# Four instead of three of the eight quads of gate and up as seven block products, and the trunk's difference block written over the block it replaces

## The chip, the cores and the metric

The kernel runs as one program on one core of a Trainium2 chip. The metric is the device time of one launch in microseconds (us). The engines that matter here are TensorE (PE: matrix products, and PEld: its weight loads), VectorE (DVE: elementwise work on two operands), ScalarE (ACT: elementwise work on one operand) and the DMA queue of SyncE (SP), which brings the weights. Each engine works through its own list of instructions in order, and the lists meet in semaphores.

## The reference, cut to what matters

A trunk of two layers over 256 tokens of width 2048. Each layer has a mixer and then a SwiGLU, and it is the SwiGLU that the change touches:

```
x = x + swiglu(rmsnorm(x, g_ffn[layer]), w_gate[layer], w_up[layer], w_down[layer])
swiglu(h, w_gate, w_up, w_down) = (silu(h @ w_gate) * (h @ w_up)) @ w_down
# h: 256 x 2048;  w_gate, w_up: 2048 x 5632;  w_down: 5632 x 2048;  all float32
```

## The kernel before, in words

**Numbers.** Every float32 operand is split into a high part that TensorE takes exactly (`wh` for weights, written by ACT at L101) and the rest (`wl`, the raw weight minus `wh`, by DVE at L102). A product is three matmuls (L207 to L209): high by high, high by low, low by high. Six buffers of 128x1024 are there for `wh` and six for `wl`; a buffer comes free when the last matmul that reads it is done. Raw weights come in pieces of 1 MB into three `raw` buffers.

**Gate and up.** The 5632 hidden columns are taken in 11 blocks of 512 (index c), in parts of 4, 4 and 3 blocks (`PARTS`); behind each part comes the down projection of its hidden columns (`token_major`: four columns of 512, 24 matmuls for every 1 MB of weights). In a block, gate and up are computed together in eight *quads* (index j), one for every 256 rows of the weights. A quad is a 2 by 2 product of blocks: two token halves by two row groups, two row groups by gate and up. An *eight* (`quad_eight`) does it in 8 block products, 24 matmuls, from two pieces of weights of 128x1024. A *seven* (`quad_seven`) does it in 7 block products, 21 matmuls, after Winograd's form of Strassen's scheme. It needs sums of weight blocks first, by DVE: t1 and t3 in one subtraction of 128x1024 (L478), t2 (L480) and t4 (L481). Then it splits four pieces: P1 (b21 and b22, straight from `raw`), P2 (t2 and t4), P3 (b11, 128x512) and P4 (t1 and t3). It needs sums of trunk blocks as well (`forms`: s1 to s4), made once a layer in `put_pair`, where the normed trunk is turned and stored in `xs`.

Three of the sums of a seven go to PSUM tiles `c11`, `c12`, `c21` (pool `mm`, 4 buffers), four to `p1`, `p6`, `p5`, `p7` (pool `sm`, 4 buffers, which the transposes use too). At the end of a block comes its *epilogue*: five copies out of PSUM by ACT (L519), eight adds of 128x512 by DVE (L520), two SiLU by ACT (L573), two products by DVE (L575). The two halves of the hidden block are then turned by 8 transposes (L241) during the next block and split again, `hid` (L581 on ACT, L582 on DVE).

**Order.** `chunks_of` prepares the weights `AHEAD` = 2 quads ahead of the products. `next_pending` puts the transposes of the block before behind the products of quad 1. The final order on each engine is fixed when the program is built, by a scheduler that may move an instruction ahead of others; the engines then keep to it. In the profile a sum of weights at L478 and one at L481 both show as L475, the line of the helper `sub`.

Of the kernel before, what the change touches and what calls it, by code (L numbers as in the profile page):

```python
# [9 lines left out]
F32R = mybir.dt.float32r  # L10
AF = mybir.ActivationFunctionType
ALU = mybir.AluOpType
AX = mybir.AxisListType

P = 128
D = 2048
T = 256
KD = D // P
# [1 line left out]
NF = DFF // P  # L20
PARTS = (4, 4, 3)

SEVEN = (3, 5, 7)
AHEAD = 2
EPS = 1e-6
NH = 16
# [6 lines left out]
def trunk(ctx: ExitStack, tc: tile.TileContext, a: dict, out: bass.AP):  # L33
    nc = tc.nc
# [13 lines left out]
    def ev(shape, dtype=F32):  # L48

        return evs.tile([P, *shape], dtype, name="ev")  # L50
# [4 lines left out]
    pending = []  # L55
# [13 lines left out]
    def gain(name, i):  # L69
        return gains[:, g_at[name] + i:g_at[name] + i + 1]  # L70
# [173 lines left out]
    def into_trunk(w, k0, nk, moving, g, sums, chunks=None, scaled=None):  # L244


        def turn(m, src):

            def put(pt):
                for j in range(2):  # L250
                    split_into(xs[:, m + j, :], pt[:, j * T:(j + 1) * T], gain(g, m + j))

            def put_pair(pt):
                xg = ev([2, T])
                for j in range(2):
                    nc.scalar.activation(out=xg[:, j, :], in_=pt[:, j * T:(j + 1) * T], func=AF.Copy, scale=gain(g, m + j))
                nc.scalar.activation(out=xs[:, m:m + 2, :T], in_=xg, func=AF.Copy)
                nc.vector.tensor_tensor(out=xs[:, m:m + 2, T:], in0=xg, in1=xs[:, m:m + 2, :T].bitcast(F32), op=ALU.subtract)
                if m // 2 not in SEVEN:
                    return  # L260
                a11, a21, a12, a22 = xg[:, 0, :P], xg[:, 0, P:], xg[:, 1, :P], xg[:, 1, P:]
                f = ev([4, P])
                s1, s2, s3, s4 = (f[:, i, :] for i in range(4))
                nc.vector.tensor_tensor(out=s1, in0=a21, in1=a22, op=ALU.add)
                nc.vector.tensor_tensor(out=s2, in0=s1, in1=a11, op=ALU.subtract)
                nc.vector.tensor_tensor(out=s3, in0=a11, in1=a21, op=ALU.subtract)
                nc.vector.tensor_tensor(out=s4, in0=a12, in1=s2, op=ALU.subtract)
                q = scaled["forms"][:, SEVEN.index(m // 2), :, :, :]
                nc.scalar.activation(out=q[:, 0, :, :], in_=f, func=AF.Copy)
                nc.vector.tensor_tensor(out=q[:, 1, :, :], in0=f, in1=q[:, 0, :, :].bitcast(F32), op=ALU.subtract)  # L270

            turned(src, put_pair if scaled else put)

        def turn_scaled(c):
            xn = []

            def two(m):
                for t in range(2 if m == 0 else 0):
                    e = ev([512])
                    nc.scalar.activation(out=e, in_=x[:, t, c * 512:(c + 1) * 512], func=AF.Copy, scale=scaled["by"][:, t:t + 1])  # L280
                    xn.append(e)
                turn(4 * c + m, lambda t, j: xn[t][:, (m + j) * P:(m + j + 1) * P])

            pending.extend([lambda: two(0), lambda: two(2)])

        def evict(c, pss):
            s = slice(c * 512, (c + 1) * 512)
            for t in range(2):
                nc.vector.tensor_tensor(out=x[:, t, s], in0=pss[t], in1=x[:, t, s], op=ALU.add)
            if g is None:  # L290
                return
            for t in range(2):
                sq = ev([512])
                nc.scalar.activation(out=sq, in_=x[:, t, s], func=AF.Square, accum_out=sums[:, t, c:c + 1])
            if g == "final":
                for t in range(2):
                    nc.vector.tensor_tensor(out=x[:, t, s], in0=x[:, t, s], in1=gfin[:, s], op=ALU.mult)
            elif scaled is None:
                for m in (4 * c, 4 * c + 2):
                    pending.append(lambda m=m: turn(m, lambda t, j: x[:, t, (m + j) * P:(m + j + 1) * P]))  # L300
            elif c == 2:
                scaled["by"], scaled["back"] = trunk_rstd(sums[:, :, :3], 1536, back=True)
                for b in range(3):
                    turn_scaled(b)
            elif c == 3:
                turn_scaled(3)

        token_major(w, k0, nk, range(4), moving, evict, chunks)
# [15 lines left out]

    def forms():

        return big.tile([P, len(SEVEN), 2, 4, P], F32R, name="ckv")


    gfin = None  # L330
# [182 lines left out]
    def feed_forward(layer, sums, scaled, g_next):  # L513
# [7 lines left out]
        for part, n in enumerate(PARTS):  # L521
            hid = hidden()
            for c in range(n):

                c11, c12, c21, c22 = (ps_mm.tile([P, 512], F32, name="mm") for _ in range(4))
                open_ = set()

                def sum_into(ps, left, right, last):
                    token_product(ps, *left, *right, id(ps) not in open_, last)
                    open_.add(id(ps))  # L530

                for j in range(KD // 2):
                    w = next(chunks)
                    lasting = j == KD // 2 - 1
                    x11, x21, x12, x22 = ((xs[:, k, t * P:(t + 1) * P], xs[:, k, T + t * P:T + (t + 1) * P])
                                          for k in (2 * j, 2 * j + 1) for t in range(2))
                    if j not in SEVEN:
                        for xk, bg, bu in (((x11, x21), "b11", "b12"), ((x12, x22), "b21", "b22")):
                            for x_t, pg, pu in ((xk[0], c11, c12), (xk[1], c21, c22)):
                                sum_into(pg, x_t, w[bg], False)  # L540
                                sum_into(pu, x_t, w[bu], pu is c22 and xk[0] is x12 and j == max(set(range(KD // 2)) - set(SEVEN)))
                    else:
                        if j == SEVEN[0]:
                            p1, p6, p5, p7 = (ps_sm.tile([P, 512], F32, name="sm") for _ in range(4))
                        q = forms[:, SEVEN.index(j)]
                        s1, s2, s3, s4 = ((q[:, 0, i, :], q[:, 1, i, :]) for i in range(4))
                        sum_into(c11, x12, w["b21"], lasting)
                        sum_into(c12, s4, w["b22"], lasting)
                        sum_into(c21, x22, w["t4"], lasting)
                        sum_into(p1, x11, w["b11"], lasting)  # L550
                        sum_into(p6, s2, w["t2"], lasting)
                        sum_into(p5, s1, w["t1"], lasting)
                        sum_into(p7, s3, w["t3"], lasting)
                    if j in (1, 2):
                        next_pending(2)
                    if j == KD // 2 - 2:
                        e22 = copy(c22)
                if f is None:
                    f = stat.tile([P, 2], F32, name="factor")
                    nc.vector.tensor_tensor(out=f, in0=trunk_rstd(sums), in1=scaled["back"], op=ALU.mult)  # L560
                e11, e12, e21, u2 = copy(c11), copy(c12), copy(c21), copy(p6)
                u4 = ev([512])
                add(e11, p1, e11)
                add(u2, p1, u2)
                add(u4, p5, u2)
                add(u2, p7, u2)
                add(e21, u2, e21)
                add(u2, p5, u2)
                add(e12, u4, e12)
                add(e22, u2, e22)  # L570
                hd = []
                for t, (g, u) in enumerate(((e11, e12), (e21, e22))):
                    nc.scalar.activation(out=g, in_=g, func=AF.Silu, scale=f[:, t:t + 1])  # L573
                    h = qpool.tile([P, 512], F32, name="qn")
                    nc.vector.scalar_tensor_tensor(out=h, in0=u, scalar=f[:, t:t + 1], in1=g, op0=ALU.mult, op1=ALU.mult)  # L575
                    hd.append(h)
                for m in (0, 2):
                    def put(pt, hid=hid, m=4 * c + m):
                        pair = hid[:, m:m + 2, :]
                        src = pt.rearrange("p (j t) -> p j t", j=2)  # L580
                        nc.scalar.activation(out=pair[:, :, :T], in_=src, func=AF.Copy)  # L581
                        nc.vector.tensor_tensor(out=pair[:, :, T:], in0=src, in1=pair[:, :, :T].bitcast(F32), op=ALU.subtract)  # L582
                    pending.append(lambda m=m, hd=hd, put=put: turned(lambda t, j: hd[t][:, (m + j) * P:(m + j + 1) * P], put))
# [240 lines left out]
```

## Time and profile before

| | |
|---|---|
| median of 3 runs | 1942.32 us (1941.19 to 1942.67) |
| the profiled execution | 1942.75 us, of which the span from first to last instruction is 1940.9 us |
| TensorE | busy 99% of the span, weight loads 83%, granted clock 0.996 |
| VectorE, ScalarE | busy 75% and 55% |
| DMA | 371 MB, 191 GB/s |

A busy share is an average over stages. A "releaser" is what ended an engine's idle time before an instruction. Instructions overlap a little at their ends, so what one of them costs its engine is read from start to start, and that is called its pitch below. Consecutive equal instructions are merged in a timeline ("x2").

### The profile page before, as it was taken

What the parts mean: (1) busy time and instruction counts of PE and PEld (TensorE: products, weight loads), DVE (VectorE), ACT (ScalarE), POOL (GpSimd) and SP (SyncE); (2) the same over time, 40 slices, a digit from 0 to 9 for tenths busy, and PEclk for the clock granted to TensorE, in tenths of its full rate; (3) what the DMA queues carried; (4) which work ended last, traced back from release to release, by engine and by line L of the source; (5) the groups of instructions that cost most, each with busy time, mean ns of one, the idle gap of its engine ahead of it and who ended that gap; (6) DMA issues with size and microseconds to landing.
All of it is one profiled execution on the core that took longest, in us unless ns stands there. A gap on an engine that the chain in (4) does not pass through costs nothing.

```text
span 1940.9 us, 23494 instructions
## 1 busy us (share of the span) xinstructions
PE 1921.9 (99%) x9110; PEld 1610.7 (83%) x9110; DVE 1448.9 (75%) x1793; ACT 1066.0 (55%) x1424; POOL 10.1 (1%) x26
## 2 busy tenths in 40 slices
PE   9999999999999999999999999999999999999997
PEld 7888888888888888888889988888888888888886
DVE  6685589985688965887676755899856889658884
ACT  6554666563456643555554755665634566435562
POOL 0000000000000000000000000000000000000000
PEclk9999999999999999999999999999999999999998
DMA  8565545565555555456455235455655556655562
GB/s 310 174 215 197 195 160 209 195 213 194 179 195 195 210 201 190 179 195 217 175 194 175 96 135 184 171 208 188 214 194 183 187 199 211 210 181 177 208 242 87
DMA packets 54688, 370.94 MB, mean 191 GB/s; under 512 B 6320, under 2 KB 7856, under 8 KB 10544
## 3 DMA queue, kind: packets, MB, share of 16 engines
q1 hardware_dynamic: 52560, 364.93, 53.5%
q10 hardware_dynamic: 2016, 4.51, 0.6%
q8 instruction: 71, 1.16, 0.2%
q14 instruction: 41, 0.34, 0.0%
HBM read 367.32 MB, written 2.10 MB: 190 GB/s over the span
## 4 chain that ended last, share of the span: by engine, by line
PE 97%; DVE 1%; DMA 1%; ACT 1%; issue 0%; POOL 0%; ACTq 0%; SPq 0%; POOLq 0%
PE mm L207 24%; PE mm L209 24%; PE mm L208 24%; PE mm L131 5%; PE sm L209 3%; PE sm L208 3%; PE sm L207 3%; PE mm L132 2%; PE sm L241 2%; PE mm L363 1%; PE mm L364 1%; PE mm L137 1%; PE mm L362 1%; PE mm L136 1%; PE mm L138 1%; DMA raw<-in_w_v 1%
## 5 line engine op out<-in xcount | busy, mean ns | idle before, releaser
L102 DVE TENSOR_TENSOR wl<-raw,wh 128x1024 fp32r<-128x1024 f32 (+1 forms) x692 | 802.7, 1165 | 342.6 <-ACT wh L101 338.9
L101 ACT ACTIVATE wh<-raw 128x1024 fp32r<-128x1024 f32 (+1 forms) x692 | 695.1, 1013 | 538.4 <-PE mm L209 458.8
L207 PE MATMUL mm<-wh,xs 128*128 128x512 f32 x1012 | 395.2, 391 | 0.0
L209 PE MATMUL mm<-wh,xs 128*128 128x512 f32 x1012 | 393.9, 389 | 0.0
L208 PE MATMUL mm<-wl,xs 128*128 128x512 f32 x1012 | 393.8, 389 | 0.0
L207 PE MATMUL mm<-wh,hid 128*128 128x512 f32 x960 | 375.5, 391 | 0.0
L209 PE MATMUL mm<-wh,hid 128*128 128x512 f32 x960 | 373.6, 390 | 0.0
L208 PE MATMUL mm<-wl,hid 128*128 128x512 f32 x960 | 373.6, 389 | 0.0
L209 PEld LDWEIGHTS mm<-wh,xs 128*128 128x128 f32 x1012 | 189.9, 188 | 39.5
L207 PEld LDWEIGHTS mm<-wh,xs 128*128 128x128 f32 x1012 | 190.0, 188 | 39.0
L208 PEld LDWEIGHTS mm<-wl,xs 128*128 128x128 f32 x1012 | 190.0, 188 | 38.8
L209 PEld LDWEIGHTS mm<-wh,hid 128*128 128x128 f32 x960 | 180.2, 188 | 37.5
L207 PEld LDWEIGHTS mm<-wh,hid 128*128 128x128 f32 x960 | 180.2, 188 | 37.0 <-ACT hid L581 0.3
L208 PEld LDWEIGHTS mm<-wl,hid 128*128 128x128 f32 x960 | 180.3, 188 | 36.7
L102 DVE TENSOR_TENSOR wl<-sums,wh 128x1024 fp32r<-128x1024 f32 x132 | 161.3, 1222 | 63.6 <-ACT wh L101 63.6
L101 ACT ACTIVATE wh<-sums 128x1024 fp32r<-128x1024 f32 x132 | 139.4, 1056 | 126.1 <-DVE sums L475 96.6
L131 PE MATMUL mm<-xs,wh 128*128 128x512 f32 x375 | 133.8, 399 | 0.0
L132 PE MATMUL mm<-xs,wl 128*128 128x256 f32 x375 | 104.8, 280 | 0.0
L131 PEld LDWEIGHTS mm<-xs,wh 128*128 128x128 f32 x375 | 70.4, 188 | 15.9 <-DVE xs L170 0.3
L475 DVE TENSOR_TENSOR sums<-raw 128x1024 f32<-128x1024 f32 x66 | 80.5, 1220 | 1.0 <-DMA raw<-in_w_gu 0.5
L520 DVE TENSOR_TENSOR ev<-sm,ev 128x512 f32<-128x512 f32 x110 | 75.6, 688 | 2.6
L207 PE MATMUL sm<-wh,ckv 128*128 128x512 f32 x198 | 77.0, 389 | 0.0
(198 smaller groups left out, 1920.2 us busy)
## 6 DMA issues: line engine op xcount, KB each, us to landing
raw<-in_w_gu SPq DMA_DIRECT2D x176, 1024.0 KB, 4.8
raw<-in_w_d SPq DMA_DIRECT2D x88, 1024.0 KB, 4.8
raw<-in_w_o SPq DMA_DIRECT2D x32, 1024.0 KB, 4.8
raw<-in_w_v SPq DMA_DIRECT2D x11, 1024.0 KB, 6.6
raw<-in_w_z SPq DMA_DIRECT2D x8, 1024.0 KB, 5.0
raw<-in_w_u SPq DMA_DIRECT2D x8, 1024.0 KB, 4.8
raw<-in_w_q SPq DMA_DIRECT2D x6, 1024.0 KB, 4.9
raw<-in_w_ckv SPq DMA_DIRECT2D x4, 1024.0 KB, 4.8
```

The lines of the kernel that those rows point to most:

```text
L101: nc.scalar.activation(out=wh[:, :m], in_=raw[:, o:o + m], func=AF.Copy)
L102: nc.vector.tensor_tensor(out=wl[:, :m], in0=raw[:, o:o + m], in1=wh[:, :m].bitcast(F32), op=ALU.subtract)
L131: nc.tensor.matmul(ps, lhsT=wh, rhs=mv, start=first, stop=False)
L132: nc.tensor.matmul(ps[:, :T], lhsT=wl, rhs=mv[:, :T], start=False, stop=last)
L136: nc.tensor.matmul(ps[:, :T], lhsT=wh, rhs=mv[:, :T], start=first, stop=False)
L137: nc.tensor.matmul(ps[:, :T], lhsT=wh, rhs=mv[:, T:], start=False, stop=False)
L207: nc.tensor.matmul(ps, lhsT=hi, rhs=wh, start=first, stop=False)
L208: nc.tensor.matmul(ps, lhsT=hi, rhs=wl, start=False, stop=False)
L209: nc.tensor.matmul(ps, lhsT=lo, rhs=wh, start=False, stop=last)
L241: nc.tensor.transpose(pt[:, o:o + P], src(t, j), ident)
L475: sub = lambda out, p, q: nc.vector.tensor_tensor(out=out, in0=p, in1=q, op=ALU.subtract)
L520: add = lambda out, p, q: nc.vector.tensor_tensor(out=out, in0=p, in1=q, op=ALU.add)
```

## The change

`SEVEN` goes from quads 3, 5, 7 to quads 2, 4, 6, 7, so that a block has four sevens and four eights. In `put_pair`, the difference s3 = a11 - a21 is written over a21 before the trunk block is split, so that `xs` holds s3 where it held x21 (which a seven doesn't use) and `forms` holds three sums instead of four. The transposes of the block before are issued behind the quad ahead of the first seven (quad 1, as before), and `c22` is copied out behind quad 5 instead of 6.

```diff
-SEVEN = (3, 5, 7)
+SEVEN = (2, 4, 6, 7)
+EIGHT = tuple(j for j in range(KD // 2) if j not in SEVEN)
...
+                seven = m // 2 in SEVEN
+                if seven:
+                    a11, a21, a12, a22 = xg[:, 0, :P], xg[:, 0, P:], xg[:, 1, :P], xg[:, 1, P:]
+                    f = ev([3, P])
+                    s1, s2, s4 = (f[:, i, :] for i in range(3))
+                    nc.vector.tensor_tensor(out=s1, in0=a21, in1=a22, op=ALU.add)
+                    nc.vector.tensor_tensor(out=s2, in0=s1, in1=a11, op=ALU.subtract)
+
+                    nc.vector.tensor_tensor(out=a21, in0=a11, in1=a21, op=ALU.subtract)
+                    nc.vector.tensor_tensor(out=s4, in0=a12, in1=s2, op=ALU.subtract)
                 nc.scalar.activation(out=xs[:, m:m + 2, :T], in_=xg, func=AF.Copy)
                 nc.vector.tensor_tensor(out=xs[:, m:m + 2, T:], in0=xg, in1=xs[:, m:m + 2, :T].bitcast(F32), op=ALU.subtract)
-                if m // 2 not in SEVEN:
+                if not seven:
                     return
-                a11, a21, a12, a22 = xg[:, 0, :P], xg[:, 0, P:], xg[:, 1, :P], xg[:, 1, P:]
-                f = ev([4, P])
...
-        return big.tile([P, len(SEVEN), 2, 4, P], F32R, name="ckv")
+        return big.tile([P, len(SEVEN), 2, 3, P], F32R, name="ckv")
...
-                                sum_into(pu, x_t, w[bu], pu is c22 and xk[0] is x12 and j == max(set(range(KD // 2)) - set(SEVEN)))
+                                sum_into(pu, x_t, w[bu], pu is c22 and xk[0] is x12 and j == EIGHT[-1])
...
-                        sum_into(p7, s3, w["t3"], lasting)
-                    if j in (1, 2):
-                        next_pending(2)
-                    if j == KD // 2 - 2:
+                        sum_into(p7, x21, w["t3"], lasting)
+                    if j == SEVEN[0] - 1:
+                        next_pending(len(pending))
+                    if j == EIGHT[-1]:
                         e22 = copy(c22)
```

The order that the scheduler makes of it changes most around the end of a block. On DVE, before, at the end of layer 0's second block, the epilogue's adds (L520) stand among the splits of eights (`wl<-raw`), and the first seven's sums begin behind seven of the eight adds:

```order
L520 TENSOR_TENSOR ev<-sm,ev 128x512
L102 TENSOR_TENSOR wl<-raw,wh 128x1024
L520 TENSOR_TENSOR ev<-sm,ev 128x512 x2
L102 TENSOR_TENSOR wl<-raw,wh 128x1024
L520 TENSOR_TENSOR ev<-sm,ev 128x512
L520 TENSOR_TENSOR ev<-ev 128x512 x2
L575 SCALAR_TENSOR_TENSOR qn<-ev,factor 128x512
L520 TENSOR_TENSOR ev<-sm,ev 128x512
L102 TENSOR_TENSOR wl<-raw,wh 128x1024
L520 TENSOR_TENSOR ev<-ev 128x512
L475 TENSOR_TENSOR sums<-raw 128x1024
L575 SCALAR_TENSOR_TENSOR qn<-ev,factor 128x512
```

And now, at the same place (the lines have moved by one to four: L524 was L520, L103 was L102, L479 and L484 were L475 and L480, L579 was L575):

```order
L103 TENSOR_TENSOR wl<-raw,wh 128x1024 x4
L524 TENSOR_TENSOR ev<-sm,ev 128x512 x2
L479 TENSOR_TENSOR sums<-raw 128x1024
L524 TENSOR_TENSOR ev<-sm,ev 128x512
L103 TENSOR_TENSOR wl<-raw,wh 128x1024
L524 TENSOR_TENSOR ev<-sm,ev 128x512
L524 TENSOR_TENSOR ev<-ev 128x512 x2
L579 SCALAR_TENSOR_TENSOR qn<-ev,factor 128x512
L524 TENSOR_TENSOR ev<-sm,ev 128x512
L484 TENSOR_TENSOR sums<-sums,raw 128x512
L524 TENSOR_TENSOR ev<-ev 128x512
L479 TENSOR_TENSOR sums<-raw,sums 128x512
```

All four split pieces of the next block's quads 0 and 1 (x4) now stand ahead of the first add, and the epilogue is interleaved with the sums and the first split of quad 2, a seven.

On ACT, at the last quad of layer 0's second block, before: the four pieces of quad 7 (`raw_2812`, `sums_2814`), then the splits for the next block, and only then, among those, the copies of `c22`, `c11` and `c12` (`mm_2602`, `mm_2599`, `mm_2600`):

```order
L101 ACTIVATE wh_2816<-raw_2812 128x1024
L101 ACTIVATE wh_2822<-sums_2814 128x1024
L101 ACTIVATE wh_2826<-raw_2812 128x512
L101 ACTIVATE wh_2830<-sums_2814 128x1024
L101 ACTIVATE wh_2857<-raw_2855 128x1024
L101 ACTIVATE wh_2861<-raw_2855 128x1024
L519 ACTIVATE ev_2889<-mm_2602 128x512
L101 ACTIVATE wh_2893<-raw_2891 128x1024
L519 ACTIVATE ev_2922<-mm_2599 128x512
L101 ACTIVATE wh_2897<-raw_2891 128x1024
L519 ACTIVATE ev_2924<-mm_2600 128x512
```

And now (quad 7 is `raw_2837` and `sums_2839`; `mm_2618`, `mm_2615`, `mm_2616` are `c22`, `c11`, `c12`):

```order
L102 ACTIVATE wh_2841<-raw_2837 128x1024
L523 ACTIVATE ev_2883<-mm_2618 128x512
L523 ACTIVATE ev_2947<-mm_2615 128x512
L523 ACTIVATE ev_2949<-mm_2616 128x512
L102 ACTIVATE wh_2847<-sums_2839 128x1024
L102 ACTIVATE wh_2851<-raw_2837 128x512
L102 ACTIVATE wh_2855<-sums_2839 128x1024
L102 ACTIVATE wh_2887<-raw_2885 128x1024
L102 ACTIVATE wh_2891<-raw_2885 128x1024
```

The copies of the finished sums now stand between the first and the second piece of quad 7. On PE two products of quad 2 (into `p5` and `p7`) are moved behind the first half of quad 3.

## Rows read from the trace of the kernel before

**Rows 1.** The page: busy time, share of the span and instructions of each engine
```profile
PE 1921.9 (99%) x9110; PEld 1610.7 (83%) x9110; DVE 1448.9 (75%) x1793; ACT 1066.0 (55%) x1424; POOL 10.1 (1%) x26
```
**Rows 2.** Busy time in stretches: block four of layer 0, then one down column
```profile
core 0: us, PE busy (x) PEld busy (x) DVE busy (x) ACT busy (x) POOL busy (x), PEclk, DMA share, GB/s
374.88:417.26 42.38, 42.38 (x193) 35.18 (x192) 38.64 (x45) 25.35 (x32) 0.00 (x0) 1.00 0.56 199
440.75:462.51 21.76, 21.76 (x97) 18.02 (x97) 11.01 (x11) 8.49 (x8) 0.00 (x0) 1.00 0.58 195
```
**Rows 3.** Timeline of PE: block two, its transposes, block four (start, us, engine, line, op)
```profile
290.97 0.39 PE L207 MATMUL mm<-wh,xs 128*128 128x512 f32 x1
...
301.85 1.03 PE L241 MATMUL sm<-ident,qn 128*128 128x128 f32 x8
...
375.71 0.39 PE L207 MATMUL mm<-wh,xs 128*128 128x512 f32 x1
```
**Rows 4.** Groups by line: the first sums of all sevens
```profile
L475 DVE TENSOR_TENSOR sums<-raw 128x1024 f32<-128x1024 f32 x66 | 80.5, 1220 | 1.0 <-DMA raw<-in_w_gu 0.5
```
**Rows 5.** Timeline of DVE: an eight's and a seven's splits, second block of layer 0
```profile
307.77 1.22 DVE L102 TENSOR_TENSOR wl<-raw,wh 128x1024 fp32r<-128x1024 f32 x1
308.91 1.22 DVE L475 TENSOR_TENSOR sums<-raw 128x1024 f32<-128x1024 f32 x1
310.05 2.35 DVE L102 TENSOR_TENSOR wl<-raw,wh 128x1024 fp32r<-128x1024 f32 x2
312.32 0.68 DVE L480 TENSOR_TENSOR sums<-sums,raw 128x512 f32<-128x512 f32 x1
313.03 0.69 DVE L475 TENSOR_TENSOR sums<-raw,sums 128x512 f32<-128x512 f32 x1
314.94 1.22 DVE L102 TENSOR_TENSOR wl<-sums,wh 128x1024 fp32r<-128x1024 f32 x1 [1.21 <-ACT wh L101]
316.08 0.68 DVE L102 TENSOR_TENSOR wl<-raw,wh 128x512 fp32r<-128x512 f32 x1
316.68 1.22 DVE L102 TENSOR_TENSOR wl<-sums,wh 128x1024 fp32r<-128x1024 f32 x1
317.81 1.22 DVE L102 TENSOR_TENSOR wl<-raw,wh 128x1024 fp32r<-128x1024 f32 x1
```
**Rows 6.** Timeline of ACT: the high part of that seven's second piece, then a copy
```profile
313.84 1.06 ACT L101 ACTIVATE wh<-sums 128x1024 fp32r<-128x1024 f32 x1 [2.99 <-DVE sums L475]
...
331.23 0.58 ACT L519 ACTIVATE ev<-mm 128x512 f32<-128x512 f32 x1
331.70 1.06 ACT L101 ACTIVATE wh<-raw 128x1024 fp32r<-128x1024 f32 x1
```
**Rows 7.** Timeline of DVE: from an epilogue's first add to the split of hid
```profile
332.51 0.68 DVE L520 TENSOR_TENSOR ev<-sm,ev 128x512 f32<-128x512 f32 x1
333.11 1.22 DVE L102 TENSOR_TENSOR wl<-raw,wh 128x1024 fp32r<-128x1024 f32 x1
...
338.76 0.75 DVE L575 SCALAR_TENSOR_TENSOR qn<-ev,factor 128x512 f32<-128x512 f32 x1
339.42 0.68 DVE L520 TENSOR_TENSOR ev<-sm,ev 128x512 f32<-128x512 f32 x1
...
346.02 1.28 DVE L582 TENSOR_TENSOR hid<-sm,hid 128x512 fp32r<-128x512 f32 x2
347.29 1.23 DVE L102 TENSOR_TENSOR wl<-sums,wh 128x1024 fp32r<-128x1024 f32 x1
```
**Rows 8.** Timeline of DVE in the first block: trunk sums and an idle time
```profile
260.77 1.23 DVE L102 TENSOR_TENSOR wl<-sums,wh 128x1024 fp32r<-128x1024 f32 x1 [2.46 <-ACT wh L101]
...
264.45 0.28 DVE L264 TENSOR_TENSOR ev<-ev 128x128 f32<-128x128 f32 x1
264.65 1.22 DVE L102 TENSOR_TENSOR wl<-raw,wh 128x1024 fp32r<-128x1024 f32 x1
```
**Rows 9.** DMA issues: the weights of gate and up, median us to landing
```profile
raw<-in_w_gu SPq DMA_DIRECT2D x176, 1024.0 KB, 4.8
```

More of the change, by code (lines that the diff above doesn't have):

```diff
@@ L256, in put_pair @@
                     nc.scalar.activation(out=xg[:, j, :], in_=pt[:, j * T:(j + 1) * T], func=AF.Copy, scale=gain(g, m + j))
+                seven = m // 2 in SEVEN
[7 more added lines that the diff above has]
+                    nc.vector.tensor_tensor(out=s4, in0=a12, in1=s2, op=ALU.subtract)
                 nc.scalar.activation(out=xs[:, m:m + 2, :T], in_=xg, func=AF.Copy)
                 nc.vector.tensor_tensor(out=xs[:, m:m + 2, T:], in0=xg, in1=xs[:, m:m + 2, :T].bitcast(F32), op=ALU.subtract)
-                if m // 2 not in SEVEN:
+                if not seven:
                     return
-                a11, a21, a12, a22 = xg[:, 0, :P], xg[:, 0, P:], xg[:, 1, :P], xg[:, 1, P:]
-                f = ev([4, P])
[L263 to L267, printed above, removed]
                 q = scaled["forms"][:, SEVEN.index(m // 2), :, :, :]
@@ L545, in feed_forward @@
                         q = forms[:, SEVEN.index(j)]
-                        s1, s2, s3, s4 = ((q[:, 0, i, :], q[:, 1, i, :]) for i in range(4))
+                        s1, s2, s4 = ((q[:, 0, i, :], q[:, 1, i, :]) for i in range(3))
                         sum_into(c11, x12, w["b21"], lasting)
```

## The prediction

> **What bounds the kernel now.** I read the page's busy times first, then the same by stages, then the timelines of the engines that look full there. Over the whole span TensorE is the full engine: 99% busy, against 75% for DVE [rows 1]. By stages it looks different. In a block of gate and up DVE is busy 38.64 us of 42.38, in a down column 11.01 of 21.76 [rows 2]: the 75% is a mean over 91% and 51%, and the change works only where DVE is at 91%.
>
> TensorE's side of a block: from the start of block two to its transposes PE runs two eights, 48 matmuls, in 301.85 - 290.97 = 10.88 us, 0.2267 us each. Two blocks take 375.71 - 290.97 = 84.74, 42.37 each [rows 3]. The 183 matmuls of a block (5 x 24 + 3 x 21) make 41.49, which leaves 0.88 for the 8 transposes. So PE never waits there, and sets the pace.
>
> DVE's side. From the last split of one eight (307.77) to that of the next (317.81) lies one seven and one eight, 10.04 us, of which 1.21 is idle [rows 5]. The idle time is a relay: DVE makes t4 (313.03), ACT makes its high part (313.84, after it had waited 2.99 us for that sum) [rows 6], and DVE takes the low part at 314.94, 1.91 us after it began t4. Nothing else of DVE's list may pass. The parts by pitch: 1.14 us for 128x1024 (307.77 to 308.91), 0.60 for 128x512 (316.08 to 316.68) [rows 5]. So an eight costs DVE 2 x 1.14 = 2.28 and a seven 10.04 - 2.28 = 7.76, the relay included. On PE they cost 24 x 0.2267 = 5.44 and 4.76. A seven saves PE 0.68 us and costs DVE 5.48 more than the eight that it replaces; the question is only whether DVE has that to spare.
>
> **The change part by part.** *The products.* 66 sevens in 22 blocks [rows 4] become 88: PE loses 22 x 3 matmuls, 22 x 0.68 = 15.0 us. A block's PE work is then 41.69 us.
>
> *DVE's list of a block*, from the first add of an epilogue to the next one, in the new order. Quad 2, a seven, is now woven into the epilogue: 8 adds at 0.60 (332.51 to 333.11) and one product at 0.66 (338.76 to 339.42) [rows 7], the sum of 1024 and the split of P1 at 1.14, t2 at 0.60: 4.80 + 0.66 + 2.28 + 0.60 = 8.34 to the start of t4. Then the relay of 1.91, in which the second product fits. Then P2, P3, P4 at 1.14, 0.60, 1.14: 13.13. Quad 3, an eight: 15.41. The two splits of hid, 347.29 - 346.02 = 1.27 [rows 7]: 16.68. Quads 4 and 5: 10.04. Quads 6 and 7, two sevens running: 2 x 7.76 = 15.52. Quads 0 and 1 of the next block: 4.56. Sum 46.80 us, against 41.69 of PE. So where the list runs without a lead it is DVE that sets a block, and the block is 46.80 - 42.37 = 4.43 longer than now.
>
> The idle part of this is three relays of 1.21 and 0.64 in the epilogue: 4.27. It is the term not seen under this load; its ends are nothing (other work fills every wait; 42.53 for a block) and the full 4.27. I take the full value, because in the new order too the split of P2 stands right behind t4 in quads 4, 6 and 7, and in the row the engine idled just so.
>
> *The lead.* In a down column DVE has half its time free [rows 2], so each part begins with all six buffers full. First blocks (one in each of the three parts of each layer, six in all) have no epilogue in their list: 46.8 - 8 x 0.60 - 2 x 0.66 - 1.27 = 39.4 us, under PE's. They win 0.68 each. At the end of one, the last split for the next block's quad 1 needs the buffer of quad 7's P2, whose last reader is the fifth of seven products, 1.36 us before the block's end. ACT and DVE take about 1.0 and 1.14 for the split, with 0.2 to 0.3 for signals and then the last copies: the first adds go 1.3 us after the block's end. Before the change they went 0.8 before it (332.51, against 290.97 + 42.37 = 333.34) [rows 3, 7].
>
> In the steady state the adds come later. PE's last wait in a block is for the low part of quad 7's P2; 12 matmuls are left then, 2.72 us. DVE has P3, P4 and two eights left, 0.60 + 1.14 + 4.56 = 6.30. So the next epilogue starts 3.58 us after the block's end. Second blocks (six) begin with 1.3 in the place of 3.58 and so take 46.80 - 2.28 = 44.52, +2.15 each. Later blocks (2 + 2 + 1 in a layer, ten in all) take +4.43.
>
> *ACT's new order.* In quad 7 the copies of c11 and c12 stand ahead of the second piece. ACT can then split P2 only after PE has finished c12: 1.36 us into quad 7, about 0.35 for the result to land, 0.47 for the copy (331.23 to 331.70) [rows 6]. DVE's own t4 comes at about that time in the steady state, so I add nothing; alone it would hold PE about 2.7 us in a block, which is the stall that the list above already gives to quad 7.
>
> *Trunk sums.* A fourth pair per layer takes three or four DVE instructions of 0.20 (264.45 to 264.65) more and a split. The idle 2.46 us there hides it [rows 8]; without that cover it would cost some 1.4 us a layer. *Down projection.* An epilogue of 10.5 us behind a lag of 3.6 ends 14 us into a down column of 21.8, and the transposes stand later on PE by then. I take nothing; up to 1 us for each of six parts is in the range.
>
> **Sum.** 6 x (-0.68) + 6 x 2.15 + 10 x 4.43 = -4.1 + 12.9 + 44.3 = +53.1. The profiled execution's own time is 1942.75 us, 0.43 over the median: 1942.32 + 53.1 = 1995.4, I say **1996 us**. Its own range: the lag after a first block between 0.3 and 3.6 (six times) and half a microsecond on the list (sixteen times), 1982 to 2010.
>
> **The rivals.** *TensorE stays the bound.* Then the 15.0 us come off: 1927.3. For it speaks the page [rows 1]. The Trainium skill (Perfetto Trace Analysis, "Identifying the Most-Contended Engine") says to improve the engine with the highest occupancy, judging TensorE by its weight loads: 83% here against DVE's 75%, and by that rule the time would be this 1927.3. The stage disagrees: 35.18 us of weight loads against 38.64 of DVE in a block [rows 2]. It holds only if DVE finds 5.1 us in a block. Chance 0.05.
>
> *The waits are filled.* If ACT works so far ahead that no relay shows, DVE's list is 42.53, 0.84 over PE's 41.69. The lead of 3.58 - 1.3 = 2.28 us covers that for two blocks behind a first one. Time: 22 x (-0.68) and a few tenths in the last blocks, about 1929; with half the relays filled (44.7 a block, +2.3 in later blocks, nothing in second ones) 1942.3 - 4.1 + 23 = 1961. Against it: the sum t4 comes out of DVE itself right before. Chance 0.05 for the first, 0.06 for the second.
>
> *A ring of buffers is longer than DVE's list.* The transposes of hid hold two of four PSUM tiles until DVE has split them, 16.7 us into its list; now quad 2 needs those tiles, and its last two products wait. From there PE has 6 matmuls, half of quad 3 (2.72), quads 4, 5, 6 (14.96) and two products; then come a copy, a split on ACT and the remaining 7.4 of DVE: 16.7 + 1.4 + 2.7 + 15.0 + 1.4 + 1.9 + 7.4 = 46.5. That is only 0.3 under the list. A raw buffer is freed about 7 us before it is wanted, and a piece lands in 4.8 [rows 9]. If one of the two is 1.5 us longer than I count, sixteen blocks carry it: 2020. Chance 0.09.
>
> *The change doesn't do what it says*: no; the order shows 22 sevens more.
>
> **How the numbers follow.** The forecast has 0.75. The range 1958 to 2020 leaves out the two gains (0.10) and the far ends. "Same" (within 0.2%, 3.9 us, which is what a measurement of this kernel can tell from no change) lies between cases and gets 0.03; faster 0.10; slower 0.87.
>
> **What would show it right or wrong.** In the profile after: blocks of about 41.7, 44.5, 46.8, 46.8 us in a part of four, read from the transposes or the SiLUs; PE idle in front of quad 7's second piece, waiting for DVE's low part or ACT's high part; DVE over 90% busy in second to fourth blocks with idle times of 1.2 only behind t4; down columns unchanged at 21.8. It is wrong if second and later blocks take 42 us, if DVE's idle time behind t4 is gone, or if PE's wait is mostly for PSUM tiles or for `raw`.

## The result and the profile after

The changed kernel takes 2001.28 us in the median of four runs (2001.0 to 2004.2), the kernel before 1942.49 in the same comparison: a ratio of 1.0307, with a 95% interval of 1.0291 to 1.0322. 1996 had been forecast: slower, as forecast, and 5 us more than forecast. The profiled spans are 1999.4 and 1940.9 us, 58.5 apart.

Lines of the file moved by a few: what was L102 (low part), L475 (first sum), L480 (t4), L520 (epilogue's adds), L207 to L209 (three matmuls of a product) before is L103, L479, L484, L524, L208 to L210 now. First the page: the busy times, then the chain of work that ended last, by engine.

```profile
PE 1941.5 (97%) x9044; PEld 1601.0 (80%) x9044; DVE 1535.2 (77%) x1913; ACT 1094.0 (55%) x1470; POOL 10.1 (1%) x26
...
PE 62%; DVE 26%; issue 5%; ACT 4%; DMA 2%; ACTq 0%; SPq 0%; POOL 0%; POOLq 0%; DVEq 0%
```

PE has 66 matmuls less (9110 - 9044) and is busy 19.6 us longer than before [rows 1]; part of that is the granted clock, below. Over the whole span it still looks like the full engine, as DVE's 77% looks like room to spare. On the page only the chain tells that DVE carries a quarter of the time.

The same by stages: the gate and up blocks of the three parts of layer 0, with the columns as in [rows 2].

```profile
249.45:431.93 182.48, 174.97 (x754) 139.31 (x753) 163.76 (x194) 109.96 (x142) 0.69 (x1) 0.98 0.49 174
519.71:698.16 178.45, 171.86 (x747) 137.83 (x745) 158.19 (x177) 102.08 (x124) 0.00 (x0) 0.99 0.50 177
785.92:919.15 133.23, 128.85 (x559) 103.62 (x557) 117.25 (x130) 77.06 (x94) 0.00 (x0) 0.99 0.50 178
```

In the kernel before the same three stretches, cut at the same matmuls, are these, PE busy to the last hundredth:

```profile
248.37:418.09 169.72, 169.72 (x767) 140.88 (x765) 150.26 (x175) 105.29 (x133) 0.69 (x1) 1.00 0.53 189
506.09:674.95 168.86, 168.86 (x759) 140.06 (x757) 146.26 (x161) 98.09 (x118) 0.00 (x0) 1.00 0.54 192
762.94:889.43 126.49, 126.49 (x568) 104.88 (x566) 107.63 (x118) 72.78 (x87) 0.00 (x0) 1.00 0.54 190
```

The stretches became 12.8, 9.6 and 6.7 us longer; with layer 1 (11.8, 9.6, 6.7) that is 57.2 of the 58.5. A down stretch between them takes 87.8 us where it took 88.0. So the time is lost where the change is, and but for 1.3 us there alone.

The pace is DVE's. The first add of each epilogue of layer 0's first part, in DVE's timeline (start, length, line; what follows in brackets is the idle time before):

```profile
293.77 0.68 DVE L524 TENSOR_TENSOR ev<-sm,ev 128x512 f32<-128x512 f32 x1
...
340.56 0.68 DVE L524 TENSOR_TENSOR ev<-sm,ev 128x512 f32<-128x512 f32 x1
...
387.34 0.69 DVE L524 TENSOR_TENSOR ev<-sm,ev 128x512 f32<-128x512 f32 x1
...
434.13 0.68 DVE L524 TENSOR_TENSOR ev<-sm,ev 128x512 f32<-128x512 f32 x1
```

They are 46.79, 46.78 and 46.79 us apart; 42.37 before. The only idle times in the middle one of these cycles stand behind t4, in the epilogue 0.55, in quads 4, 6 and 7 1.20, 1.21 and 1.18; 4.14 together. The one of quad 7, and what DVE does behind it until the next epilogue:

```profile
376.06 1.22 DVE L479 TENSOR_TENSOR sums<-raw 128x1024 f32<-128x1024 f32 x1
377.32 0.69 DVE L484 TENSOR_TENSOR sums<-sums,raw 128x512 f32<-128x512 f32 x1
378.05 0.69 DVE L479 TENSOR_TENSOR sums<-raw,sums 128x512 f32<-128x512 f32 x1
379.92 1.23 DVE L103 TENSOR_TENSOR wl<-sums,wh 128x1024 fp32r<-128x1024 f32 x1 [1.18 <-ACT wh L102]
381.06 0.69 DVE L103 TENSOR_TENSOR wl<-raw,wh 128x512 fp32r<-128x512 f32 x1
381.66 1.22 DVE L103 TENSOR_TENSOR wl<-sums,wh 128x1024 fp32r<-128x1024 f32 x1
382.80 4.63 DVE L103 TENSOR_TENSOR wl<-raw,wh 128x1024 fp32r<-128x1024 f32 x4
```

ACT meanwhile: the copies of c11 and c12, then the high part of the sums, held up by t4 and not by the copies (0.24 us, releaser DVE). PE waits for that high part once in each of sixteen blocks, all but the first of a part. Below stand two rows of ACT, then two of PE, then the group of all such waits in the page.

```profile
377.31 1.28 ACT L523 ACTIVATE ev<-mm 128x512 f32<-128x512 f32 x2 [2.39 <-PE mm L210]
378.83 1.06 ACT L102 ACTIVATE wh<-sums 128x1024 fp32r<-128x1024 f32 x1 [0.24 <-DVE sums L479]
```
```profile
379.94 0.50 PE L208 MATMUL mm<-wh,xs 128*128 128x512 f32 x1 [1.98 <-ACT wh L102]
380.28 0.39 PE L208 MATMUL sm<-wh,ckv 128*128 128x512 f32 x1
```
```profile
L208 PE MATMUL mm<-wh,xs 128*128 128x512 f32 x880 | 342.1, 395 | 28.7 <-ACT wh L102 28.3
```

That is a chain of DVE (t4), ACT (high part), PE, with DVE idle for 1.2 us of it. The 28.3 us are not the loss: PE waits there because DVE's list is behind, and what PE waits in one place it does not wait in another.

### The profile page after: what moved, and what is told of

The parts are those of the page before. It is cut to its first block, busy times and chain, and to the rows that moved or that the text cites. A ratio compares the mean times of both kernels' runs of the same rounds, so it can differ in the third digit from the quotient of the medians.

```text
span 1999.4 us, 23599 instructions
## 1 busy us (share of the span) xinstructions
PE 1941.5 (97%) x9044; PEld 1601.0 (80%) x9044; DVE 1535.2 (77%) x1913; ACT 1094.0 (55%) x1470; POOL 10.1 (1%) x26
## 4 chain that ended last, share of the span: by engine, by line
PE 62%; DVE 26%; issue 5%; ACT 4%; DMA 2%; ACTq 0%; SPq 0%; POOL 0%; POOLq 0%; DVEq 0%
PE mm L209 15%; PE mm L210 15%; PE mm L208 15%; DVE wl L103 14%; DVE sums L479 4%; PE mm L132 4%; ACT wh L102 4%; DVE ev L524 3%; PE mm L133 2%; DVE sums L484 2%; PE sm L209 2%; PE sm L210 2%; PE sm L208 1%; DMA raw<-in_w_v 1%; DVE hid L586 1%
## 5 line engine op out<-in xcount | busy, mean ns | idle before, releaser
L103 DVE TENSOR_TENSOR wl<-raw,wh 128x1024 fp32r<-128x1024 f32 (+1 forms) x692 | 785.1, 1147 | 283.7 <-ACT wh L102 282.0
L102 ACT ACTIVATE wh<-raw 128x1024 fp32r<-128x1024 f32 (+1 forms) x692 | 676.7, 994 | 447.0 <-PE mm L210 360.8
L208 PE MATMUL mm<-wh,hid 128*128 128x512 f32 x960 | 375.1, 391 | 0.9 <-ACT hid L585 0.9
L209 PE MATMUL mm<-wl,hid 128*128 128x512 f32 x960 | 374.9, 391 | 0.0
L210 PE MATMUL mm<-wh,hid 128*128 128x512 f32 x960 | 374.2, 390 | 0.0
L208 PE MATMUL mm<-wh,xs 128*128 128x512 f32 x880 | 342.1, 395 | 28.7 <-ACT wh L102 28.3
L209 PE MATMUL mm<-wl,xs 128*128 128x512 f32 x880 | 349.7, 397 | 6.1 <-DVE wl L103 5.1
L210 PE MATMUL mm<-wh,xs 128*128 128x512 f32 x880 | 345.3, 392 | 0.0
L102 ACT ACTIVATE wh<-sums 128x1024 fp32r<-128x1024 f32 x176 | 185.5, 1054 | 231.7 <-DVE sums L479 200.1
L103 DVE TENSOR_TENSOR wl<-sums,wh 128x1024 fp32r<-128x1024 f32 x176 | 215.2, 1223 | 94.9 <-ACT wh L102 94.9
L208 PEld LDWEIGHTS mm<-wh,xs 128*128 128x128 f32 x880 | 165.3, 188 | 68.9 <-ACT wh L102 35.1
L208 PEld LDWEIGHTS mm<-wh,hid 128*128 128x128 f32 x960 | 180.3, 188 | 38.1 <-ACT hid L585 1.4
L209 PEld LDWEIGHTS mm<-wl,xs 128*128 128x128 f32 x880 | 165.8, 188 | 56.2 <-DVE wl L103 23.9
L210 PEld LDWEIGHTS mm<-wh,hid 128*128 128x128 f32 x960 | 180.3, 188 | 37.3
L209 PEld LDWEIGHTS mm<-wl,hid 128*128 128x128 f32 x960 | 180.4, 188 | 36.7
L210 PEld LDWEIGHTS mm<-wh,xs 128*128 128x128 f32 x880 | 166.1, 189 | 32.3
L479 DVE TENSOR_TENSOR sums<-raw 128x1024 f32<-128x1024 f32 x88 | 107.2, 1218 | 0.9 <-DMA raw<-in_w_gu 0.4
L523 ACT ACTIVATE ev<-mm 128x512 f32<-128x512 f32 x88 | 50.8, 586 | 52.4 <-PE mm L210 51.4
L524 DVE TENSOR_TENSOR ev<-sm,ev 128x512 f32<-128x512 f32 x110 | 73.6, 683 | 0.2
```

The lines of the kernel that those rows point to most:

```text
L102: nc.scalar.activation(out=wh[:, :m], in_=raw[:, o:o + m], func=AF.Copy)
L103: nc.vector.tensor_tensor(out=wl[:, :m], in0=raw[:, o:o + m], in1=wh[:, :m].bitcast(F32), op=ALU.subtract)
L208: nc.tensor.matmul(ps, lhsT=hi, rhs=wh, start=first, stop=False)
L209: nc.tensor.matmul(ps, lhsT=hi, rhs=wl, start=False, stop=False)
L210: nc.tensor.matmul(ps, lhsT=lo, rhs=wh, start=False, stop=last)
L479: sub = lambda out, p, q: nc.vector.tensor_tensor(out=out, in0=p, in1=q, op=ALU.subtract)
```

## The experiments

All but one are edits of the changed kernel; times beside them are of the same comparisons, where the kernel before ran at 1942.5 to 1942.8 us.

**Is it the fourth seven, or the rest of the edit?** The rest is the trunk's differences stored in place and the order that comes with it. (With three sevens the same code puts the transposes behind quad 2 and copies `c22` behind quad 6.)

```
-SEVEN = (2, 4, 6, 7)
+SEVEN = (3, 5, 7)
```

> The changed kernel with SEVEN = (3, 5, 7) again: only the difference stored in xs, the earlier sums in put_pair and the order around them stay. If DVE's list of a block is the cause, three sevens bring it back to about 41.4 us, under TensorE's 42.4: 1942 us, within 4. If the trunk's sums (made ahead of the split of xs, written in place) or the place of the transposes cost the time, a good part of the 59 us stays: 1960 us or more.

Measured: 1943.05, ratio 1.0002 [0.9992, 1.0011]. The stretches are those of before (168.86 and 126.49). The storing in place costs nothing; all is in the fourth seven and the places of the sevens, which this run does not separate.

**TensorE's buffers and products, or the sums on VectorE?** The matmuls of the changed kernel stay, the sums of weight blocks go; t1 to t4 are then split from raw weights in their place, so a part of the computation is left out.

```
-        sub(sums[:, :1024], raw[:, 512:1536], raw[:, :1024])
...
-        sub(t4, b[3], t2)
-        parts += split_raw(sums[:, 1024:], 1024)
+        parts += split_raw(raw[:, 1024:], 1024)
...
-        parts += split_raw(sums[:, :1024], 1024)
+        parts += split_raw(raw[:, :1024], 1024)
```

> The changed kernel without the sums of weight blocks: P2 and P4 are split from raw weights instead of t2, t4, t1, t3 (that part of the computation is left out); matmuls, splits and the epilogue stay. DVE's list falls by 3 x 3.74 + 2.99 = 14.2 us to about 32.6 a block, TensorE's 41.7 rule: the 15 us come off, 1927 to 1931 us. If TensorE waits for PSUM tiles held by the transposes, or for ACT's copies ahead of quad 7's second piece, the blocks stay near 46: 1985 us or more.

Measured: 1927.24, ratio 0.9924 [0.9909, 0.9938]. This is the gain of the products alone, and it came to 15.5 us (15.0 had been worked out from three matmuls in 22 blocks). PSUM tiles, raw buffers and ACT's copies are as in the changed kernel and hold up nothing here. By itself that does not exclude the ring of buffers, because DVE's work is a part of that ring and is shorter in this run too. But in the changed kernel PE's waits in these blocks are for weights (28.3 us for ACT's high parts, 5.1 for DVE's low parts) and, 2.0 us of them, of transposes for DVE's products; the profile puts none down to a PSUM tile or to `raw`. The next run leaves tiles and buffers as they are.

**How much of the loss is the relay?** In each seven the two sums that t4 needs go first, and the split of the raw half is issued behind t4. While ACT makes t4's high part, DVE then has that split to do. (The split is tied to t4, because the scheduler may move an instruction ahead of others.)

```
-        parts = split_raw(raw[:, 1024:], 1024)
         nc.vector.tensor_tensor(out=t2, in0=t3, in1=b[0], op=ALU.add)
-        sub(t4, b[3], t2)
+        last = sub(t4, b[3], t2)
+        with tc.issue_after(last.ins):
+            parts = split_raw(raw[:, 1024:], 1024)
```

> The changed kernel with the split of P1's low part queued on DVE behind the sum t4, so that it runs while ACT makes P2's high part. The same instructions, no work less. If DVE's list with its relays sets the block: the list falls by 3 x 1.14 + 0.65 = 4.1 us to 42.7, lag over TensorE's 41.7 grows by 1 us a block and the lead of 2.3 covers most of it: 1928 to 1938 us. If only DVE's work counted and the relays were filled already: no change, 2001 us. If PSUM tiles or ACT's copies set the block: within 10 us of 2001.

Measured: 1936.92, ratio 0.9971 [0.996, 0.9982]. Not an instruction fewer (DVE executes 1913, as in the changed kernel) and 64 us faster. DVE's timeline in quad 7 now (t2 is L483 here, and the epilogue's adds are L525):

```profile
365.76 1.22 DVE L479 TENSOR_TENSOR sums<-raw 128x1024 f32<-128x1024 f32 x1
367.02 0.69 DVE L483 TENSOR_TENSOR sums<-sums,raw 128x512 f32<-128x512 f32 x1
367.75 0.69 DVE L479 TENSOR_TENSOR sums<-raw,sums 128x512 f32<-128x512 f32 x1
368.36 1.22 DVE L103 TENSOR_TENSOR wl<-raw,wh 128x1024 fp32r<-128x1024 f32 x1
369.63 1.23 DVE L103 TENSOR_TENSOR wl<-sums,wh 128x1024 fp32r<-128x1024 f32 x1
370.78 0.68 DVE L103 TENSOR_TENSOR wl<-raw,wh 128x512 fp32r<-128x512 f32 x1
```

The bracket with the 1.2 us is gone. The adds of the epilogues are 43.13 us apart, from the second block of a part on:

```profile
333.91 0.69 DVE L525 TENSOR_TENSOR ev<-sm,ev 128x512 f32<-128x512 f32 x1
...
377.06 1.28 DVE L525 TENSOR_TENSOR ev<-sm,ev 128x512 f32<-128x512 f32 x2
```

A stretch of four blocks takes 167.79 us where it took 178.45 (before: 168.86). 46.78 - 43.13 = 3.65 of the 4.14 idle us of a cycle were won. Most of the rest is in these rows too: the sums' split starts 1.27 us after the raw one (368.36, 369.63), where 1.14 is the pitch, so 0.13 is left of the relay in each of three sevens; in the fourth a product of the epilogue stands between.

**The dose, from the other side.** In the kernel before, each seven's first sum is made twice.

```
         sub(sums[:, :1024], raw[:, 512:1536], raw[:, :1024])
+        sub(sums[:, :1024], raw[:, 512:1536], raw[:, :1024])
```

> The kernel before with one more VectorE instruction per seven (the subtraction of 1024 of L478, 1.14 us, issued twice with the same result), so 3.42 us more per block and not a matmul more. Theory (VectorE's in-order list bounds a block as soon as it is longer than TensorE's 42.37): the list of before is 41.4, it becomes 44.8, the steady cycle from block to block 44.8, ten later blocks of 2.4 and six second blocks of 0 to 2: 1962 to 1980. Rival (TensorE, 99% busy, is the bound and VectorE at 74% has room): 1942, no change.

Measured: 1971.21, ratio 1.0147 [1.0132, 1.0162]. Its later epilogues stand 44.99 and 45.15 apart, against 44.8 from the list. The kernel before had been less than 1 us per block from the point at which DVE takes over (1.0 by the list's 41.4 of 42.37, 0.6 to 0.8 by the measured cycles less 3.42); a stretch went from 168.86 to 174.27, with TensorE's work untouched.

**Another placement: three sevens at the end of a block.**

```
-SEVEN = (2, 4, 6, 7)
+SEVEN = (3, 5, 6, 7)
```

> The changed kernel with the four sevens at quads 3, 5, 6, 7. DVE's list has the same instructions and the same relays but one may be covered by the splits of hid: 45.5 to 46.8 a block, 1980 to 2003 us. If the PSUM tiles are the cause (the first seven stands right behind the transposes), it has an eight in between now, 5.4 us: then TensorE would wait less and the time would be under 1960 us.

Measured: 2040.35, ratio 1.05 [1.0484, 1.0516]. Both theories missed, the one that the other runs bear out by 37 us. The sums are the same and the matmuls are the same. A stretch of four took 187.01 us (178.45 in the changed kernel), 8.56 more. The rows of the first block of layer 0's second part, DVE's first add and PE's first matmul of the next block, tell a good part of it:

```profile
568.05 0.68 DVE L524 TENSOR_TENSOR ev<-sm,ev 128x512 f32<-128x512 f32 x1
```
```profile
565.22 0.39 PE L208 MATMUL mm<-wh,xs 128*128 128x512 f32 x1
```

and the same two in the changed kernel:

```profile
559.91 0.68 DVE L524 TENSOR_TENSOR ev<-sm,ev 128x512 f32<-128x512 f32 x1
```
```profile
560.74 0.39 PE L208 MATMUL mm<-wh,xs 128*128 128x512 f32 x1
```

With three sevens in a row, DVE ends even a first block 2.83 us behind PE, where it had been 0.83 ahead. The 8.56 us are: 0.54 in the first block itself, 3.66 of lead lost (2.83 + 0.83), 2.81 in the three cycles (47.68, 48.45 and 48.17 against 47.93, 46.78 and 46.78) and 1.55 at the end, where the last epilogue began 1.69 us behind the block instead of 3.24. Of the cycles' part, 0.65 in a cycle is the fourth relay, which stood in the epilogue in the changed kernel and cost 0.55 there; now all four cost 1.2 (4.79 idle, against 4.14). Two of the three cycles hold something more, the granted clock. PE waits in quad 6 already, the clock falls behind that wait, and PE is late with c12; ACT's copies of c11 and c12, which stand ahead of the high part of the sums, then hold that high part up, and DVE idles for 1.97 us instead of 1.18. The granted clock is 0.50 from 649.0 to 652.4. A row of ACT behind it and one of DVE:

```profile
654.51 1.28 ACT L523 ACTIVATE ev<-mm 128x512 f32<-128x512 f32 x2 [4.01 <-PE mm L210]
```
```profile
656.76 1.23 DVE L103 TENSOR_TENSOR wl<-sums,wh 128x1024 fp32r<-128x1024 f32 x1 [1.97 <-ACT wh L102]
```

So the new order on ACT, which costs nothing in the changed kernel (0.24 us to spare), costs 0.5 to 0.8 us in such a cycle.

**Relays or the run of sevens?** The same placement in the kernel with the filled relay.

```
-SEVEN = (2, 4, 6, 7)
+SEVEN = (3, 5, 6, 7)
```

> The sevens at 3, 5, 6, 7 (as in e5, 2040) with the relay filled (as in e3, 1937). Theory A (both the relay and the run of three sevens at a block's end count: in e5 the first block of a part already leaves VectorE 2.8 us late, where the changed kernel leaves it 0.8 us early): the cycle falls from 47.7 to 43.2, three later blocks of a part at 43.3 behind a first of 42.3, 172 per stretch of four against 167.8 in e3: 1950 to 1970. Theory B (e5 lost by the relays alone, none of its four standing in a block's end): 1935 to 1942.

Measured: 1954.64, ratio 1.0062 [1.0047, 1.0077], inside theory A and outside B. The relays were 86 of the 98 us by which e5 was above the kernel before; but with the relay gone the run of sevens still costs 18 us against e3 (1936.92): its stretch of four is 170.68 against 167.79. DVE ends a first block 2.36 us behind PE (551.51, 549.15), where in e3 it is 0.83 ahead. The reading is that three sevens in a row take 3 x (7.76 - 1.21) = 19.7 us on DVE's list and 14.3 on PE, and that the lead of two or three weight chunks does not cover the difference. The first seven has moved from quad 2 to quad 3 as well, with the transposes one quad later; no run tests that by itself.

**Taking more off VectorE: GpSimd.** In e3, the three adds of an epilogue that read no PSUM go to GpSimd.

```
+        held = lambda out, p, q: nc.gpsimd.tensor_tensor(out=out, in0=p, in1=q, op=ALU.add)
...
-                add(e21, u2, e21)
+                held(e21, u2, e21)
...
-                add(e12, u4, e12)
-                add(e22, u2, e22)
+                held(e12, u4, e12)
+                held(e22, u2, e22)
```

> The changed kernel with the relay filled (as in e3) and the three adds of a block's end that touch no PSUM on GpSimd instead of VectorE. Theory: VectorE's cycle of 43.13 loses 3 x 0.60 = 1.8 and falls to 41.3, under TensorE's 41.7; TensorE bounds every block and the time is 1928 to 1933. Rivals: GpSimd's add is slow or holds VectorE up (its only adds seen are 128x2 at 0.69 us), then the multiplications behind it (L579) wait on VectorE's queue and the time is 1937 to 1960, as e3 or worse; or TensorE's idle of e3 is not VectorE's, then 1937.

Measured: 1983.59, ratio 1.0213 [1.0196, 1.023]; the second of the outcomes, and beyond its end. The rows of GpSimd and of DVE in one epilogue (L526 is the add that GpSimd makes, L581 DVE's product):

```profile
337.95 2.85 POOL L526 TENSOR_TENSOR ev<-ev 128x512 f32<-128x512 f32 x2 [38.23 <-DVE ev L525]
342.03 1.68 POOL L526 TENSOR_TENSOR ev<-ev 128x512 f32<-128x512 f32 x1 [1.23 <-DVE ev L525]
```
```profile
338.32 0.68 DVE L525 TENSOR_TENSOR ev<-sm,ev 128x512 f32<-128x512 f32 x1
339.59 1.76 DVE L581 SCALAR_TENSOR_TENSOR qn<-ev,factor 128x512 f32<-128x512 f32 x1 [0.58 <-POOL ev L526]
...
341.87 0.68 DVE L479 TENSOR_TENSOR sums<-raw,sums 128x512 f32<-128x512 f32 x1
342.47 2.32 DVE L103 TENSOR_TENSOR wl<-raw,wh 128x1024 fp32r<-128x1024 f32 x1
344.71 0.74 DVE L581 SCALAR_TENSOR_TENSOR qn<-ev,factor 128x512 f32<-128x512 f32 x1
```

An add takes GpSimd 1.58 us in the mean (DVE's pitch is 0.60). The two DVE instructions on SBUF alone that begin while such an add runs are 1.0 and 1.1 us longer: 1.76 against 0.74, 2.32 against 1.22. One that reads PSUM (338.32) and one that began before the add (341.87) are not. So DVE saves 1.8 us in a block and loses 0.58 + 1.0 + 1.1 = 2.7 again; its cycle is 43.99, against 43.13. The epilogue gets longer as well, and that reaches PE twice. At the start of a down column the transposes wait for it (429.05, 1.56; 432.62, 1.53), so that a down stretch takes 91.3 us instead of 87.8, and with the two shorter ones of the third parts (3.0 and 1.4 more) the six are 18.6 us longer. And in later blocks PE waits up to 1.3 us for the split of hid; the gate and up stretches are 3.6 to 4.7 us longer, 26.0 in all. These two are 44.6 of the 44.8 us between the two profiled spans. The Trainium skill (Perfetto Trace Analysis, "Optimizing Scalar/DVE Operations") warns that moving work between GpSimd and VectorE may not help since they share a read port of SBUF. The trace agrees, with the 1.0 and 1.1 us.

**A version with less on VectorE where it runs late.** In e3, quad 6 is an eight in the third block of each part of four, with its trunk difference in a place of its own.

```
-SEVEN = (2, 4, 6, 7)
-EIGHT = tuple(j for j in range(KD // 2) if j not in SEVEN)
+ALWAYS = (2, 4, 7)
+EXTRA = 6
...
+def sevens(n, i):
+    return ALWAYS if n == 4 and i == 2 else tuple(sorted(ALWAYS + (EXTRA,)))
...
-                    todo.append((wgu[c, j], quad_seven if j in SEVEN else quad_eight))
+                    todo.append((wgu[c, j], quad_seven if j in sevens(n, c - at) else quad_eight))
```

> The kernel of e3 with quad 6 as an eight in the third block of each part of four (its trunk difference in a place of its own). VectorE's lists there lose 3.3, TensorE's gain 0.68 us, in 4 blocks. Theory (what e3 has above the 1927 of the kernel without sums is VectorE's 43.13 in later blocks against TensorE's 41.6): a stretch of four blocks falls from 167.8 to 167.0, the first of a layer from 169.1 to 167.8 or so, 1932 to 1936. Rival (the rest of e3's loss is not VectorE's list): the added products alone show, 4 x 0.68 on 1936.9, 1938 to 1941.

> The kernel of e3 again, on the same chip as e8 and in more rounds: 1936 to 1938, 0.2 to 0.4% under the kernel before, if its gain is real; within 0.1% of it if it was chance.

Measured: e8 1935.27, ratio 0.996 [0.9946, 0.9974]; e9, the kernel of e3 again, 1936.56, ratio 0.9967 [0.9955, 0.998]. The gain of the filled relay is real: twice 0.3%, with both intervals below 1. The stretches of e8 went the way of the theory, 167.15 against 167.79 in the second parts and 168.27 against 169.04 in the first part of layer 0, but not in that of layer 1 (169.05 against 168.97). The two intervals, both taken against the kernel before, overlap widely; the times themselves don't (e8 1934.6 to 1936.3, e9 1936.5 to 1936.9, five each), so a gain of 1 us or so is likely and no more is shown. Either is faster than both kernels.

## Why the prediction was right, and where its sizes were off

**DVE's list sets the block: right, to a hundredth.** 46.80 us had been added up from pitches of the kernel before; 46.78 and 46.79 were measured. Its most uncertain term, the idle time behind t4, was taken at its full end, 4.27; it is 4.14, with 0.55 in the epilogue (0.64 forecast); the rest of the list is 42.64, where 42.53 was forecast. That these two errors cancel to a hundredth is luck; that each is near 0.1 is not. e3 shows that it was that term which decided: 3.65 us less of it in a cycle, 64 us less in the time.

**The products: right.** 15.0 us by count, 15.5 in e2.

**First blocks: right in four of six.** PE ran them 0.68 us shorter than before in the second and third parts of both layers, as forecast, 0.25 and 0.15 in the first parts. Sum -3.1, forecast -4.1.

**Second blocks: the right sum from wrong parts.** +2.15 was forecast for each. In second and third parts it was +1.42 to +1.46, because the lag behind a first block was taken too long. DVE's first add stood 0.83 us ahead of the block's end (559.91, 560.74). A split for the next block (1.14) stands behind it there and makes the cycle 47.93 instead of 46.78 (the next add is at 607.84), so counted in the forecast's order the epilogue began 0.3 behind the block's end, not 1.3.

In the first part of each layer it was +4.70 and +4.15: there DVE ended the first block 1.97 us late (293.77, against 291.80), so it began the second without a lead. (Of the two numbers, 1.6 and 1.0 are a fall of the clock, see below, which the next block gives back.) The lateness comes from a term that the prediction put at nothing. Its list of a first block, 39.4, should have been 40.1, since the second product of an epilogue fills a relay and saves nothing when it goes; above all it holds no work for the trunk, whose sums were taken as hidden. But in the first block of a layer DVE also makes the sums and splits of the trunk's last two pairs, both of them sevens now, and they stand behind the idle time, not in it:

```profile
263.42 0.28 DVE L263 TENSOR_TENSOR ev<-ev 128x128 f32<-128x128 f32 x1
...
265.29 1.22 DVE L103 TENSOR_TENSOR wl<-raw,wh 128x1024 fp32r<-128x1024 f32 x1
266.42 0.69 DVE L269 TENSOR_TENSOR xs<-ev,xs 128x512 fp32r<-128x512 f32 x1
...
268.56 1.22 DVE L103 TENSOR_TENSOR wl<-sums,wh 128x1024 fp32r<-128x1024 f32 x1
```

263.42 to 265.29 and 266.42 to 268.56 are 4.0 us that the first blocks of other parts don't have. Net of what DVE idles more there, 2.6 are left: from quad 4's first sum to the first add it is 35.67 us here (258.10 to 293.77) and, with the same splits counted, 33.06 there (527.99 to 559.91, and 1.14 for the split behind the add). No run takes this work out by itself. In e3 it is there too and doesn't make DVE late: with the relays filled, DVE's first add is 0.83 us ahead in all six first blocks. Second blocks together: +14.6, forecast +12.9.

**Later blocks: right in the mean, spread by something not foreseen.** Forecast +4.43 ten times, 44.3; measured 45.7. One by one they are +2.9 and +4.9 to +6.0, although DVE's cycle is 46.78 to 46.80 in all of them. PE's wait in quad 7, nearly 2 us, was forecast; what the clock did behind it was not. Stretches of the changed kernel, the last column but two being the granted clock: right behind such waits in blocks two, three and four of the first part, then in the third block of the second part and in the last of the third.

```profile
333.20:338.40 5.20, 4.96 (x13) 3.60 (x14) 5.20 (x6) 5.20 (x7) 0.00 (x0) 0.67 0.43 145
380.30:385.50 5.20, 4.96 (x22) 3.72 (x21) 5.20 (x6) 5.20 (x7) 0.00 (x0) 1.00 0.52 170
427.00:430.60 3.60, 3.60 (x10) 2.41 (x10) 3.60 (x4) 3.60 (x5) 0.00 (x0) 0.53 0.30 55
...
647.00:652.92 5.92, 5.46 (x15) 3.98 (x16) 5.72 (x6) 5.92 (x9) 0.00 (x0) 0.71 0.47 162
...
913.50:919.15 5.65, 5.42 (x16) 3.92 (x16) 5.65 (x6) 5.65 (x8) 0.00 (x0) 0.70 0.51 173
```

After the waits of 1.98 us at 333.16 and 1.99 at 647.22 the clock fell to its lower level for some microseconds: 13 matmuls fall into 5.2 us, where 22 did when it had not fallen (380.30). It fell so behind eight of the twelve waits of 1.96 to 1.99 us, and behind none of the four of 1.13 to 1.18 (those of the second blocks of second and third parts). Each fall costs PE 1.7 us (5.20 at 0.67), the eight 14. That is less than half of why PE is busy 19.6 us longer with 66 matmuls (15.0 us) fewer; the larger part is at the full clock, where PE starts matmuls more than 0.227 us apart and the profile does not call it idle (379.94 to 380.28). Inside a part of the changed kernel a fall costs nothing, because DVE is the one waited for: the next cycle is 46.78 all the same, the block is longer and the next shorter. (In e5 a fall did lengthen DVE's cycle.) Where it meets the last block of a part, the down column begins later. In the first part the last epilogue began 2.20 us behind the block's end (431.93 to 434.13), in the second, without a fall, 3.24 (698.16 to 701.40): 1.0 us lost; in the third parts, behind a fall, it began 1.7 behind: 1.6 lost in each. In three of six last blocks this makes some 4.1 us in all.

**The sum.** Blocks: -3.1 + 14.6 + 45.7 = +57.2, forecast +53.1. Outside them +1.3: 1.1 us ahead of the first block (its stretch starts at 249.45, before at 248.37), 1.0 in the last down stretch, where PE waits 0.9 us for a split of `hid`, 0.9 won in the others. Together 58.5, 5.4 over the forecast: 1.0 in first blocks, 1.7 in second, 1.4 in later ones, 1.3 outside. Sorted by cause it is 4.1 from the falls of the clock, which were not foreseen, and 1.3 outside. Without the falls the blocks come to 53.0, beside the forecast's 53.1: the later ones to 44.1 of 44.3, the second ones to 12.0 of 12.9 and the first to -3.1 of -4.1. The later ones are the mechanism; that the errors of first and second blocks cancel (the trunk's work against the lag) is luck.

**The rivals.** *TensorE stays the bound* (1927.3): that is what e2 gives, and only with the sums left out. *The waits are filled* (1929): not in the changed kernel, but it is a fair forecast of the kernel in which they are filled, 1936.9; it missed that the list without idle time comes to 43.13 rather than 42.53. *A ring of buffers* (2020): the profile puts no wait of PE down to a PSUM tile or to `raw` in the changed kernel's blocks, and e3, with the same buffers, is 64 us faster. The rule of the Trainium skill that the prediction weighs (Perfetto Trace Analysis, "Identifying the Most-Contended Engine") would still name TensorE, taken over the whole span (80% weight loads, 77% DVE). The runs disagree: filling DVE's waits in this kernel gave 64 us.

**What stays open.** Why the clock falls after one wait of 1.98 us and not after the next; how much of e7's 18 us is the run of three sevens and how much the later place of the first.

## What to carry to other kernels

Compare engines stage by stage, and add up the in-order list of each with its idle times: an exchange of a little work on the full engine for much on the next one pays only up to the point where the second list is as long, here less than 1 us away. Before work is taken out of such a list, look for a relay in it (one engine makes a value, another converts it, the first takes it back) and put independent work of the same engine between; here that was worth 64 us without an instruction less. Spread the items that are heavy on the second engine over a block: with two of them at its end DVE was 0.83 us ahead after a first block (e3), with three 2.36 behind (e7).

## What the runs showed of the hardware that had not been expected

- Eight of twelve waits of 1.96 to 1.99 us on TensorE were followed by a fall of the granted clock (0.53 to 0.71 over 3.6 to 5.9 us in the stretches above) to the lower of its two levels (1.2 GHz), in the rows of the matmuls 0.42 us from one to the next (335.14, 335.56, 335.99) where 0.227 is usual. After the other four, and after four waits of 1.13 to 1.18 us, the clock stayed at 1.00.
- A fall cost the changed kernel nothing inside a part, where DVE's cycle set the pace, and 0.5 to 0.8 us of a cycle in e5, where ACT's copies of PE's results stand in front of what DVE waits for.
- GpSimd's add of 128x512 took 1.58 us in the mean. Two DVE instructions on SBUF that began beside it were 1.0 and 1.1 us longer than alone; one that reads PSUM was not.
